# Second norm of a tile issued whole, with the operands of the tile ahead of it in mid-slot; last norms spread to the end

## The chip, the cores and the metric

The kernel runs on one core of one Trainium2 chip. The metric is the device time of one execution in microseconds. Five engines work in parallel, each in the order of its own instruction stream: TensorE (PE, with its weight loads shown apart as PEld), VectorE (DVE), ScalarE (ACT), GpSimd (POOL) and SyncE (SP), which issues the transfers here.

## The reference

One decoder layer for a prompt of 2048 rows and a sample group of 8 × 4 = 32 rows, which share the weights. The model width is 1024 (`D`). After the attention heads and the spatial-gating units, which this change does not touch, come

```
x = x + concat(att, u * gate) @ w_out                  # output projection, residual
h = rmsnorm(x, norm2_g)
x = x + (silu(h @ w_gate) * (h @ w_up)) @ w_down       # SwiGLU, width 2816
y = rmsnorm(x, final_g)
rmsnorm(x, g) = x * rsqrt(mean(x * x) + eps) * g
```

All of it is in fp32; the kernel returns `y` and the key, value and gating caches.

## The kernel before, in words

The 2048 rows are 16 row tiles of 128 rows (`P`), the sample group is one tile of 32. They go through the output projection, the second norm and the SwiGLU in three blocks: 6 tiles, 6 tiles, and 4 tiles with the sample tile ahead of them. Precise fp32 products are made of three matmuls each, of operands that are split into a high and a low part (`hi`, `lo`): the high part is a copy in the multiplier's format on ACT, the low part a subtraction on DVE or POOL. The products of the SwiGLU and of the last projection go through a seven-product scheme for 2 × 2 blocks, so that their operands are also sums and differences of quarters.

**The second phase.** For each block, `second_phase` (L2167) goes once over the block's tiles in an `order`; one turn is called a slot here. In slot k, PE computes the second half of the output projection of tile `order[k]`: twice 12 matmuls (`out_part`, L1436 to L1438) into one PSUM bank `ps_o`. Around them stands `norm2_slot` (L1545), which is issued at the start of the slot and takes two tiles on by one stage each:

- the tile of one slot ago, `order[k-1]`, has its *norm* done: the bank is added to the residual (`out_end`, L1447, DVE; where the first half of the projection is still in its bank, that is added first), POOL multiplies by the gain (L1473), ACT squares and sums (L1480 or L1483), DVE makes the mean (L1456, L1457), ACT the root (L1458), DVE a Newton step (L146 to L150), and ACT scales the tile in place (L1488);
- the tile of two slots ago, `order[k-2]`, becomes *operands* (`Operands`, L1490): PE transposes its eight 128 × 128 pieces into two PSUM banks `ps_t` (L1500), and ACT and DVE (POOL for one subtraction) make from them the sums and the high and low parts. `first` holds L1514 to L1520, `second` the first split (L139, POOL's L142) and L1525, `third` the second split (L139, DVE's L142), `last` the subtraction L1533, which is the last to read the second bank.

The two are issued in an interleaved order: eviction and gain, transposes and `first`, square, `second`, mean, root and Newton step, `third`, scaling, `last`. `ps_t` takes its banks in turn from a ring of two, so the next tile's transposes need the bank that L1533 reads last.

At each half slot `tick()` runs the jobs that were put there by `later(...)`: the weights of the coming SwiGLU are copied to the high part on ACT (`high`, L1619) and subtracted on POOL (`low_half`, L1623). After the last slot, one more `norm2_slot` and the last tile's operands run within the SwiGLU's first steps.

**The last projection.** `Down` multiplies with `w_down` and makes the final norm. Its `run` goes over steps n; at each, `split` prepares the operands of three steps later (L1883 and L1884 on ACT, L1885 and L1886 on DVE), `mats` issues 12 matmuls, and `queue` holds the norm steps of finished tiles (`late_half`, L1940): square, mean, root, scaling of one half with the gain (DVE), scaling of the other half (ACT), output (SP). For the last four even tiles (`quick`) the six steps stand at n + 1, 2, 2, 3, 3, 4. The last three steps are done by `tail` (L1995), one row tile m after the other (PE order by m); then come the four last odd tiles with their eviction (L1920), square (L1927), mean, root, Newton step, scaling (L2017 on ACT, L2018 on DVE with the gain) and two transfers each, one tile after the other.

Of the kernel before, what the change touches and what calls it, by code (L numbers as in the profile page):

```python
# [10 lines left out]
F32 = mybir.dt.float32  # L11
F32R = mybir.dt.float32r
AF = mybir.ActivationFunctionType
OP = mybir.AluOpType
# [5 lines left out]
P = 128  # L20
T = 2048
NT = T // P
D = 1024
# [11 lines left out]
EPS = 1e-6  # L35
# [31 lines left out]
def hymba_step(ctx: ExitStack, tc: tile.TileContext, A: dict, O: dict):  # L67
# [110 lines left out]
    def zn_tile():  # L178
        return rp.tile([P, 512], F32, name="zn", tag="zn", bufs=3)
# [1264 lines left out]
    def out_end(B, i, half, ps):  # L1444
        hs = slice(half * 512, (half + 1) * 512)
        if B.rows[i] == P:
            dve.tensor_add(B.acc[i][:, hs], B.acc[i][:, hs], ps)  # L1447
# [12 lines left out]
    def rms_c(s1, n):  # L1460
        v, r = s1[:n, 1:2], s1[:n, 2:3]
        newton(r, v)
        return r
# [6 lines left out]
    def norm2_gain(B, i):  # L1470
        n = B.rows[i]
        B.xn[i] = square_tile() if n == P else fa.tile([P, D], F32, name="xns", tag="acc5")
        pool.tensor_mul(B.xn[i][:n], B.acc[i][:n], gain[0][:n])  # L1473
# [12 lines left out]
    def norm2_scale(B, i, r):  # L1486
        n = B.rows[i]
        act.activation(B.xn[i][:n], B.xn[i][:n], AF.Copy, scale=r)  # L1488
# [46 lines left out]
    def place_staged(B):  # L1535

        for z, eng in enumerate((act, dve)):
# [4 lines left out]
            else:  # L1542
                act.activation(dst, src, AF.Copy)

    def norm2_slot(B, k, order):  # L1545

        n = len(order)
        cur = order[k - 1] if 1 <= k <= n else None
        x = None
        if k == n and B.last:  # L1550
            place_staged(B)
        if cur is not None:
            if cur in B.open:
# [272 lines left out]
    class Down:  # L1826
# [95 lines left out]
        def behind(self, k, fn, *args):  # L1922
            self.queue.setdefault(self.n + k, []).append((fn, args))

        def square(self, i, c):
            x = self.acc[i][:, c * 512:(c + 1) * 512]
            act.activation(zn_tile(), x, AF.Square, accum_out=self.sq[i][:, (0, 3)[c == i % 2]:][:, 0:1])  # L1927

        def early_half(self, i):

            self.sq[i] = self.p2.tile([P, 4], F32, name="sq", tag="sq", bufs=8)
            c = i % 2
            x = self.acc[i][:, c * 512:(c + 1) * 512]
            self.behind(1, self.square, i, c)
            self.behind(1, pool.tensor_mul, x, x, gain[1][:, c * 512:(c + 1) * 512])

        def late_half(self, i, quick=False):
            steps = (1, 2, 2, 3, 3, 4) if quick else (1, 2, 3, 4, 5, 6)
            for k, fn in zip(steps, (self.late_square, self.mean, self.root, self.scale, self.scale_rest, self.out)):
                self.behind(k, fn, i)  # L1940

        def late_square(self, i):
            self.square(i, 1 - i % 2)

        def mean(self, i):
            s1 = self.sq[i]
            dve.tensor_scalar(s1[:, 0:1], s1[:, 0:1], s1[:, 3:4], None, op0=OP.add)
            dve.tensor_scalar(s1[:, 1:2], s1[:, 0:1], 1.0 / D, EPS, op0=OP.mult, op1=OP.add)

        def root(self, i):  # L1950
            act.activation(self.sq[i][:, 2:3], self.sq[i][:, 1:2], AF.Sqrt)

        def scale(self, i):
            r = rms_c(self.sq[i], P)
            cs = slice((1 - i % 2) * 512, (2 - i % 2) * 512)
            x = self.acc[i][:, cs]
            dve.scalar_tensor_tensor(x, x, r, gain[1][:, cs], op0=OP.mult, op1=OP.mult)

        def scale_rest(self, i):
            x = self.acc[i][:, i % 2 * 512:(i % 2 + 1) * 512]  # L1960
            act.activation(x, x, AF.Copy, scale=self.sq[i][:, 2:3])

        def out(self, i):
            for c in (i % 2, 1 - i % 2):
# [3 lines left out]
        def run(self):  # L1968
            self.queue = {}
            for n in range(2 * NS - TAIL):  # L1970
                self.n = n
                hv, s, j = self.at(n)
                tick()
                self.sums(n + 3)
                self.split(n + 3)
                self.load(n + 6)
                if s in (0, 2) and j in (5, 8):
                    self.acc_loads(hv, s // 2, j // 8)
                if s > 2 and n % 2 == 0 and n < NS + 5 * NJ:
                    roll(1)  # L1980
                self.mats(n)
                wide = not (hv and s == 6)
                m = j // 2 if wide else j
                if n >= NJ and m < 4 and not (wide and j % 2):
                    phv, ps_, _ = self.at(n - j - 1)
                    self.evict(phv, ps_, m, self.prev)
                    i = phv * 8 + 2 * m
                    if ps_ in (1, 4):
                        self.early_half(i + ps_ // 4)
                    elif ps_ in (5, 6):  # L1990
                        self.late_half(i + ps_ - 5, not wide)
                for fn, args in self.queue.pop(n, ()):
                    fn(*args)  # L1993
                if j == NJ - 1:
                    self.prev = self.banks  # L1995
            self.tail()

        def tail(self):
            n0 = 2 * NS - TAIL
            for _ in range(4):  # L2000
                tick()
            for n in sorted(self.queue):
                for fn, args in self.queue[n]:
                    fn(*args)

            def begin(m):
                i = 8 + 2 * m + 1
                self.mean(i)
                self.root(i)

            def root_end(m):
                return rms_c(self.sq[8 + 2 * m + 1], P)

            def finish(m, r):
                i = 8 + 2 * m + 1
                x = self.acc[i]
                act.activation(x[:, 512:], x[:, 512:], AF.Copy, scale=r)  # L2017
                dve.scalar_tensor_tensor(x[:, 0:512], x[:, 0:512], r, gain[1][:, 0:512], op0=OP.mult, op1=OP.mult)  # L2018
                self.out(i)
# [12 lines left out]
            begin(3)  # L2032
            finish(3, root_end(3))

    def second_part(B, h):

# [36 lines left out]
    gain = []  # L2073
# [21 lines left out]
    def open_end(B, i):  # L2095
        out_end(B, i, 0, B.open.pop(i))
# [379 lines left out]
```

## Time and profile before

| | |
|---|---|
| runs, median of 3 | 2480.85 us (2478.23 to 2482.76) |
| profiled execution | 2477.78 us, its span 2476.0 us |
| mean granted clock of PE | 0.993 of full speed |
| busy share of the span | PE 97%, PEld 86%, DVE 68%, ACT 49%, POOL 49% |
| the places of the change | second phases: 943.9 to 984.5 us, 1372.8 to 1401.6 and 1782.5 to 1803.8 (block 0, 1, 2); the end: 2447 to 2476 us |

A line of the timeline gives start and duration in us, engine, line of the kernel, operation, output<-inputs, form and count; in brackets stands the idle time just before, with the engine, tile and line that ended it. A matmul of 128 × 512 shows 0.39 us, since matmuls overlap; their starts are some 0.23 us apart. The trace is of one execution, so sums are made against its own time.

### The profile page before, as it was taken

The numbers are of one execution on the slowest core, as the hardware profiler recorded it, in microseconds if no ns is written. First come the engines' busy times: TensorE is split into PE (matmuls) and PEld (weight loads), VectorE is DVE, ScalarE is ACT, GpSimd is POOL, SyncE is SP. The second block draws the span as 40 slices with busy tenths as digits, with TensorE's granted clock in tenths as the row PEclk, the third lists the DMA queues.
The fourth block names the chain that finished last, engine by engine and source line by source line (L and its number), as shares of the span: only waits on it lengthen the run. The fifth ranks groups of instructions, "written<-read, shape, count | busy, mean of one in ns | idle before, by whom it ended". The sixth has DMA issues, their size and how long they took to land. (4 is left out here: it accounts for less than half of the span.)

```text
span 2476.0 us, 39227 instructions
## 1 busy us (share of the span) xinstructions
PE 2394.6 (97%) x13358; PEld 2123.2 (86%) x13358; DVE 1694.0 (68%) x3093; ACT 1223.0 (49%) x2421; POOL 1209.2 (49%) x921
## 2 busy tenths in 40 slices
PE   8999999999989889999999999999999999999997
PEld 7787787778888777999998899999799998888886
DVE  4369786446878777655665687776567666877886
ACT  6424344546877666433333533334455554445544
POOL 1145653224575756666664576667468872100100
PEclk9999999999999999999999999999999999999999
DMA  8873854788788765566669166766747676766842
GB/s 265 250 209 114 285 146 144 238 278 266 231 281 260 226 179 179 178 212 212 207 204 312 46 238 246 258 233 220 264 145 235 220 229 250 267 197 234 297 135 88
DMA packets 316949, 537.17 MB, mean 217 GB/s; under 512 B 28609, under 2 KB 151906, under 8 KB 310862
## 3 DMA queue, kind: packets, MB, share of 16 engines
q1 hardware_dynamic: 311788, 526.16, 64.8%
q10 hardware_dynamic: 4962, 8.51, 1.2%
q8 instruction: 106, 1.74, 0.3%
q14 instruction: 93, 0.76, 0.1%
HBM read 418.41 MB, written 186.28 MB: 244 GB/s over the span
## 5 line engine op out<-in xcount | busy, mean ns | idle before, releaser
L1686 PE MATMUL ps_m<-xh,op 128*128 128x384 f32 (+5 forms) x1932 | 612.2, 317 | 0.3 <-DVE raw L1723 0.2
L1687 PE MATMUL ps_m<-xl,op 128*128 128x384 f32 (+5 forms) x1932 | 611.9, 317 | 0.0
L1688 PE MATMUL ps_m<-xh,op 128*128 128x384 f32 (+5 forms) x1932 | 611.3, 316 | 0.0
L1623 POOL TENSOR_TENSOR op<-fr,op 128x512 fp32r<-128x512 f32 x286 | 403.2, 1426 | 90.0 <-ACT op L1619 67.3
L1686 PEld LDWEIGHTS ps_m<-xh,op 128*128 128x128 f32 x1932 | 363.9, 188 | 1.6 <-DVE raw L1723 0.6
L1687 PEld LDWEIGHTS ps_m<-xl,op 128*128 128x128 f32 x1932 | 363.8, 188 | 0.6
L1688 PEld LDWEIGHTS ps_m<-xh,op 128*128 128x128 f32 x1932 | 364.2, 189 | 0.0
L1623 POOL TENSOR_TENSOR op<-pair,op 128x512 fp32r<-128x512 f32 x126 | 169.0, 1342 | 157.3 <-DVE hr L1748 85.0
L335 PE MATMUL ps_s<-wh,xh 128*128 128x512 f32 x480 | 196.2, 409 | 6.2 <-ACT xh L139 6.2
L1619 ACT ACTIVATE op<-fr 128x512 fp32r<-128x512 f32 x330 | 196.5, 621 | 9.7 <-DMA fr<-ab_d 5.8
L336 PE MATMUL ps_s<-wl,xh 128*128 128x512 f32 x480 | 190.1, 396 | 0.0
L337 PE MATMUL ps_s<-wh,xl 128*128 128x512 f32 x480 | 189.8, 395 | 0.0
L1737 ACT ACTIVATE ps_t<-zn 128x384 f32<-128x384 f32 (+2 forms) x132 | 60.0, 454 | 249.7 <-DVE zn L1716 204.9
L1883 ACT ACTIVATE op<-fr 128x512 fp32r<-128x512 f32 x140 | 88.7, 634 | 181.7 <-issue 88.0
L1993 POOL TENSOR_TENSOR ac<-ac,final_g 128x512 f32<-128x512 f32 x12 | 19.5, 1622 | 319.6 <-ACT zn L1927 252.7
L1885 DVE TENSOR_TENSOR op<-fr,op 128x512 fp32r<-128x512 f32 x140 | 102.2, 730 | 75.3 <-ACT op L1883 75.2
L1619 ACT ACTIVATE op<-pair 128x512 fp32r<-128x512 f32 x126 | 79.0, 627 | 110.2 <-DVE pair L1609 110.2
L335 PEld LDWEIGHTS ps_s<-wh,xh 128*128 128x128 f32 x480 | 91.9, 191 | 34.6 <-issue 7.3
L337 PEld LDWEIGHTS ps_s<-wh,xl 128*128 128x128 f32 x480 | 91.7, 191 | 20.5 <-DVE xl L142 0.2
L1900 PE MATMUL ps_m<-op 128*128 128x512 f32 x280 | 108.9, 389 | 0.0
L1901 PE MATMUL ps_m<-op 128*128 128x512 f32 x280 | 108.9, 389 | 0.0
L1902 PE MATMUL ps_m<-op 128*128 128x512 f32 x280 | 108.9, 389 | 0.0
(553 smaller groups left out, 5965.0 us busy)
## 6 DMA issues: line engine op xcount, KB each, us to landing
fr<-in_w_gate_dram SPq DMA_DIRECT2D x132, 256.0 KB
out_ks_dram<-in_cache_k_dram SPq DMA_DIRECT2D x56, 512.0 KB
out_vs_dram<-in_cache_v_dram SPq DMA_DIRECT2D x56, 512.0 KB
fr<-in_w_up_dram SPq DMA_DIRECT2D x110, 256.0 KB
fr<-ab_d SPq DMA_DIRECT2D x88, 256.0 KB
a<-h_d SPq DMA_DIRECT2D x80, 256.0 KB
fr<-t_d SPq DMA_DIRECT2D x80, 256.0 KB
raw<-in_w_in_dram SPq DMA_DIRECT2D x72, 256.0 KB
```

The costliest lines, as they stand in the source:

```text
L335: pe.matmul(o[j], xh[:, k, :], wh, start=(k == 0), stop=False)
L336: pe.matmul(o[j], xh[:, k, :], wl, start=False, stop=False)
L337: pe.matmul(o[j], xl[:, k, :], wh, start=False, stop=(k == KD - 1))
L1619: act.activation(ops[f, j][0], ab[f][j], AF.Copy)
L1623: (eng or pool).tensor_sub(lo_, ab[f][j], hi.bitcast(F32))
L1686: pe.matmul(out, wh[:, ks], xh[:, :, k], start=(k == 0), stop=False)
L1687: pe.matmul(out, wh[:, ks], xl[:, :, k], start=False, stop=False)
L1688: pe.matmul(out, wl[:, ks], xh[:, :, k], start=False, stop=(k == 3))
L1885: dve.tensor_sub(wl, w, wh.bitcast(F32))
L1900: pe.matmul(banks[m], hh[:, ts], wh, start=first, stop=False, skip_group_check=more)
L1901: pe.matmul(banks[m], hh[:, ts], wl, start=False, stop=False, skip_group_check=more)
L1902: pe.matmul(banks[m], hl[:, ts], wh, start=False, stop=j == NJ - 1, skip_group_check=more)
```

## The change

1. `second_phase`: in all slots but the last, the interleaved `norm2_slot` is replaced. At the start of slot k, `norm2_sum` issues the whole norm of `order[k-1]`; between the two halves of 12 matmuls `norm2_operands` issues the transposes and the whole operands of `order[k-2]`. The last slot and the call after it keep `norm2_slot`.
2. `Down.late_half`: without `quick`, every tile has one step per n, at n + 1 to n + 6.
3. `tail`: the four last odd tiles are taken in pairs. Their sums lie beside each other in one tile `[P, 4, 2]`, and mean, root and Newton step are done on 128 × 2 elements (`roots(0)`, `roots(2)`). POOL multiplies the low columns by the gain after the square, DVE then scales them alone; most outputs move behind the last matmuls.

```diff
+    def norm2_sum(B, cur):
+        if cur in B.open:
+            open_end(B, cur)
+        out_end(B, cur, 1, B.half1.pop(cur))
+        norm2_gain(B, cur)
+        s1, more = norm2_square(B, cur, None)
+        rms_b(s1, B.rows[cur], more)
+        norm2_scale(B, cur, rms_c(s1, B.rows[cur]))
+
+    def norm2_operands(B, i):
+        x = Operands(B, i)
+        x.first()
+        x.second()
+        x.third()
+        x.last()
...
         def early_half(self, i):
 
-            self.sq[i] = self.p2.tile([P, 4], F32, name="sq", tag="sq", bufs=8)
+            if i < 8 or i % 2 == 0:
+                self.sums_tile(i)
+            elif i % 4 == 1:
+                self.sums_tile(i, i + 2)
...
-        def late_half(self, i, quick=False):
-            steps = (1, 2, 2, 3, 3, 4) if quick else (1, 2, 3, 4, 5, 6)
-            for k, fn in zip(steps, (self.late_square, self.mean, self.root, self.scale, self.scale_rest, self.out)):
-                self.behind(k, fn, i)
+        def late_half(self, i):
+            for k, fn in enumerate((self.late_square, self.mean, self.root, self.scale, self.scale_rest, self.out)):
+                self.behind(k + 1, fn, i)
...
-            r = {}
             for m in range(4):
                 for n in range(n0, 2 * NS):
                     self.mats(n, (m,))
-                if m:
-                    begin(m - 1)
-                    r[m - 1] = root_end(m - 1)
-                self.evict(1, 6, m, self.Y)
-                self.late_square(8 + 2 * m + 1)
-                if m:
-                    finish(m - 1, r[m - 1])
-            begin(3)
-            finish(3, root_end(3))
+                sum_up(m)
+                if m == 1:
+                    roots(0)
+                    self.scale_rest(tile_of(0))
+                elif m == 3:
+                    self.scale_rest(tile_of(1))
+                    for y in range(2):
+                        scale_low(y)
+                        self.out(tile_of(y))
+                    roots(2)
+            scale_low(2)
+            self.scale_rest(tile_of(2))
+            self.out(tile_of(2))
+            scale_low(3)
+            x = self.acc[tile_of(3)][:, 512:]
+            dve.tensor_scalar(x, x, self.col(tile_of(3), 2), None, op0=OP.mult)
+            self.out(tile_of(3))
...
     def second_phase(B, order, after=None):
 
         for k, i in enumerate(order):
-            norm2_slot(B, k, order)
+            apart = k < len(order) - 1
+            if not apart:
+                norm2_slot(B, k, order)
+            elif k:
+                norm2_sum(B, order[k - 1])
             B.half1[i] = ps = ps_o()
             for c in range(2):
                 tick()
+                if c and apart and k > 1:
+                    norm2_operands(B, order[k - 2])
                 if c and k > 2 and i in B.open:
                     first_end(B, i)
                 out_part(B, i, 1, range(c * 4, c * 4 + 4), ps, c == 0, c == 1)
```

The new functions in `tail` are these (`newton` is the Newton step, L146 to L155):

```diff
+            def sum_up(m):
+                self.evict(1, 6, m, self.Y)
+                self.late_square(tile_of(m))
+                x = low_columns(m)
+                pool.tensor_mul(x, x, gain[1][:, 0:512])
+
+            def roots(m):
+                t_ = self.sq[tile_of(m)][0]
+                dve.tensor_add(t_[:, 0], t_[:, 0], t_[:, 3])
+                dve.tensor_scalar(t_[:, 1], t_[:, 0], 1.0 / D, EPS, op0=OP.mult, op1=OP.add)
+                act.activation(t_[:, 2], t_[:, 1], AF.Sqrt)
+                newton(t_[:, 2], t_[:, 1])
```

The order of ACT's instructions in block 0, from slot 2 on, before (`acc_9962` is the second tile, whose norm this is; `ps_t_10274` and `ps_t_10279` hold the first tile's transposes; `s` are the sums):

```order
L1619 ACTIVATE op<-raw 128x512
L1514 ACTIVATE zn<-ps_t_10274 128x256
L1515 ACTIVATE xh_9950<-ps_t_10274 128x256
L1480 ACTIVATE xh_9950,s_10108<-acc_9962 128x512
L139 ACTIVATE xh_9950<-zn 128x512
L1525 ACTIVATE xh_9950<-ps_t_10279 128x512
L1458 ACTIVATE s_10108<-s_10108 128x1
L139 ACTIVATE xh_9950<-zn 128x512
L1488 ACTIVATE pair<-pair,s_10108 128x1024
L1619 ACTIVATE op<-fr 128x512 x2
```

And ACT in the changed kernel, at the same place (the first tile's transposes are now in `ps_t_10303` and `ps_t_10308`; the copies are now L1635):

```order
L1635 ACTIVATE op<-raw 128x512
L1480 ACTIVATE xh_9950,s_10108<-acc_9962 128x512
L1458 ACTIVATE s_10108<-s_10108 128x1
L1488 ACTIVATE pair<-pair,s_10108 128x1024
L1635 ACTIVATE op<-fr 128x512 x2
L1514 ACTIVATE zn<-ps_t_10303 128x256
L1515 ACTIVATE xh_9950<-ps_t_10303 128x256
L139 ACTIVATE xh_9950<-zn 128x512
L1525 ACTIVATE xh_9950<-ps_t_10308 128x512
L139 ACTIVATE xh_9950<-zn 128x512
L1483 ACTIVATE xh_9950,s_10348<-acc_10267 128x1024
```

The norm's three instructions (L1480, L1458, L1488) stood between those of the operands; now they stand together ahead of the operands, with the weight copies between the two, and the next norm (L1483, third tile) begins behind the operands' last. DVE's rows move alike: eviction, mean and Newton step of a tile come together, ahead of L1516 to L1533.

At the end of the program, DVE's last evictions (L1920 before, L1936 now) and what stands between them, before:

```order
L1920 TENSOR_TENSOR acc_18494<-acc_18494,ps_o_24394 128x512
L2018 SCALAR_TENSOR_TENSOR ac<-ac,sq,final_g 128x512
L1947 TENSOR_SCALAR sq<-sq 128x1
L1948 TENSOR_SCALAR sq<-sq 128x1
L146 RECIPROCAL sq<-sq 128x1
L148 TENSOR_SCALAR sq<-sq 128x1
L149 TENSOR_SCALAR sq<-sq 128x1
L150 TENSOR_SCALAR sq<-sq 128x1
L1920 TENSOR_TENSOR acc_18570<-acc_18570,ps_o_24395 128x512
```

And now:

```order
L1936 TENSOR_TENSOR acc_18494<-acc_18494,ps_o_24394 128x512
L1936 TENSOR_TENSOR acc_18570<-acc_18570,ps_o_24395 128x512
L2052 TENSOR_SCALAR ac<-ac,sq 128x512 x2
L2045 TENSOR_TENSOR sq<-sq 128x2
L2046 TENSOR_SCALAR sq<-sq 128x2
L146 RECIPROCAL sq<-sq 128x2
```

The last two evictions (tiles `acc_18494`, `acc_18570`) follow each other; the small operations of their norms come once, on two columns, behind the scaling of the two tiles before.

More of the change, by code (lines that the diff above doesn't have):

```diff
@@ L1923, in behind, with col, sums_tile @@
             self.queue.setdefault(self.n + k, []).append((fn, args))
+        def col(self, i, k):
+            t_, y = self.sq[i]
+            return t_[:, k, y:y + 1]
+        def sums_tile(self, *tiles):
+            t_ = self.p2.tile([P, 4, 2], F32, name="sq", tag="sq", bufs=8)
+            for y, i in enumerate(tiles):
+                self.sq[i] = t_, y
         def square(self, i, c):
             x = self.acc[i][:, c * 512:(c + 1) * 512]
-            act.activation(zn_tile(), x, AF.Square, accum_out=self.sq[i][:, (0, 3)[c == i % 2]:][:, 0:1])
+            act.activation(zn_tile(), x, AF.Square, accum_out=self.col(i, (0, 3)[c == i % 2]))
         def early_half(self, i):
-            self.sq[i] = self.p2.tile([P, 4], F32, name="sq", tag="sq", bufs=8)
+            if i < 8 or i % 2 == 0:
+                self.sums_tile(i)
+            elif i % 4 == 1:
+                self.sums_tile(i, i + 2)
             c = i % 2
@@ L1945, in mean @@
         def mean(self, i):
-            s1 = self.sq[i]
-            dve.tensor_scalar(s1[:, 0:1], s1[:, 0:1], s1[:, 3:4], None, op0=OP.add)
-            dve.tensor_scalar(s1[:, 1:2], s1[:, 0:1], 1.0 / D, EPS, op0=OP.mult, op1=OP.add)
+            dve.tensor_scalar(self.col(i, 0), self.col(i, 0), self.col(i, 3), None, op0=OP.add)
+            dve.tensor_scalar(self.col(i, 1), self.col(i, 0), 1.0 / D, EPS, op0=OP.mult, op1=OP.add)
         def root(self, i):
-            act.activation(self.sq[i][:, 2:3], self.sq[i][:, 1:2], AF.Sqrt)
+            act.activation(self.col(i, 2), self.col(i, 1), AF.Sqrt)
         def scale(self, i):
-            r = rms_c(self.sq[i], P)
+            newton(self.col(i, 2), self.col(i, 1))
             cs = slice((1 - i % 2) * 512, (2 - i % 2) * 512)
             x = self.acc[i][:, cs]
-            dve.scalar_tensor_tensor(x, x, r, gain[1][:, cs], op0=OP.mult, op1=OP.mult)
+            dve.scalar_tensor_tensor(x, x, self.col(i, 2), gain[1][:, cs], op0=OP.mult, op1=OP.mult)
         def scale_rest(self, i):
             x = self.acc[i][:, i % 2 * 512:(i % 2 + 1) * 512]
-            act.activation(x, x, AF.Copy, scale=self.sq[i][:, 2:3])
+            act.activation(x, x, AF.Copy, scale=self.col(i, 2))
         def out(self, i):
@@ L1990, in run @@
                     elif ps_ in (5, 6):
-                        self.late_half(i + ps_ - 5, not wide)
+                        self.late_half(i + ps_ - 5)
                 for fn, args in self.queue.pop(n, ()):
@@ L2004, in tail, with low_columns, scale_low @@
                     fn(*args)
[L2006 to L2019, printed above, removed]
-            r = {}
+            tile_of = lambda m: 8 + 2 * m + 1
+            def low_columns(m):
+                return self.acc[tile_of(m)][:, 0:512]
+            def sum_up(m):
[9 more added lines that the diff above has]
+                newton(t_[:, 2], t_[:, 1])
+            def scale_low(m):
+                x = low_columns(m)
+                dve.tensor_scalar(x, x, self.col(tile_of(m), 2), None, op0=OP.mult)
             for m in range(4):
```

## The prediction

> **What bounds the kernel now.** I read the page's first part, then TensorE's waits, then the timeline of the places that the change touches.
>
> ```profile
> span 2476.0 us, 39227 instructions
> ...
> PE 2394.6 (97%) x13358; PEld 2123.2 (86%) x13358; DVE 1694.0 (68%) x3093; ACT 1223.0 (49%) x2421; POOL 1209.2 (49%) x921
> ...
> PE ps_t L1500 <- ACT pair L1488: 3.6, 4, 1.5
> PE ps_t L1900 <- ACT op L1884: 3.2, 2, 2.7
> ...
> PE ps_t L1500 <- ACT xns L1488: 1.4, 1, 1.4
> ...
> PE ps_t L1500 <- DVE xl L1533: 0.3, 1, 0.3
> ```
>
> TensorE (PE) sets the time: it is busy for 97% of the span. A wait row reads: who waits <- for whom: total us, times, longest. PE's waits at the transposes (L1500) are 3.6 + 1.4 + 0.3 = 5.3 us over three blocks, and in the tail (L1900) 3.2 us. That is all that the change can take away directly. Whatever PE newly waits for is added to the end one for one. So the question is how long a round of ScalarE (ACT) and VectorE (DVE) lasts against a slot of PE.
>
> ```profile
> 955.02 1.03 PE L1500 MATMUL ps_t<-ident,pair 128*128 128x128 f32 x8
> 961.48 1.36 PE L1500 MATMUL ps_t<-ident,pair 128*128 128x128 f32 x8
> ...
> 976.15 1.38 PE L1500 MATMUL ps_t<-ident,pair 128*128 128x128 f32 x8 [1.29 <-ACT pair L1488]
> 983.64 1.09 PE L1500 MATMUL ps_t<-ident,pair 128*128 128x128 f32 x8 [0.54 <-ACT pair L1488]
> ```
>
> The timeline of block 0 (start, duration, engine, line): from one tile's transposes to the next, 961.48 − 955.02 = 6.46 us, are a slot: 1.03 of transposes and 24 matmuls, so (6.46 − 1.03)/24 = 0.226 each. PE needs no more, yet waits 1.29 once. Why:
>
> ```profile
> 976.08 0.68 DVE L1533 TENSOR_TENSOR xl<-ps_t,xh 128x512 fp32r<-128x512 f32 x1
> 976.68 0.67 DVE L1447 TENSOR_TENSOR acc<-acc,ps_m 128x512 f32<-128x512 f32 x1
> ...
> 982.43 1.15 ACT L1488 ACTIVATE pair<-pair,s 128x1024 f32<-128x1024 f32 x1 [0.52 <-DVE s L150]
> 982.86 0.68 DVE L1533 TENSOR_TENSOR xl<-ps_t,xh 128x512 fp32r<-128x512 f32 x1
> ```
>
> From one L1533, the last operation of a tile's operands, to the next one 982.86 − 976.08 = 6.78 us pass: that is today's round on ACT and DVE, in which the norm of one tile and the operands of the tile ahead of it fill each other's gaps. It is 0.3 longer than a slot.
>
> **The change part by part.** First, both chains alone. The first norm of the block has no operands beside it, and the last operands have no norm:
>
> ```profile
> 949.65 0.69 DVE L1447 TENSOR_TENSOR acc<-acc,ps_o 128x512 f32<-128x512 f32 x1 [1.55 <-PE ps_o L1438]
> ...
> 952.86 1.16 ACT L1488 ACTIVATE pair<-pair,s 128x1024 f32<-128x1024 f32 x1 [1.04 <-POOL pair L1473]
> 953.92 0.62 ACT L1619 ACTIVATE op<-fr 128x512 fp32r<-128x512 f32 x1
> ...
> 955.22 0.69 DVE L1447 TENSOR_TENSOR acc<-acc,ps_o 128x512 f32<-128x512 f32 x1 [0.40 <-PE ps_o L1438]
> ```
> ```profile
> 991.17 0.39 ACT L1514 ACTIVATE zn<-ps_t 128x256 f32<-128x256 f32 x1 [0.54 <-PE ps_t L1500]
> ...
> 993.89 0.60 ACT L1525 ACTIVATE xh<-ps_t 128x512 fp32r<-128x512 f32 x1 [0.22 <-DVE zn L1520]
> ...
> 996.43 0.61 ACT L139 ACTIVATE xh<-zn 128x512 fp32r<-128x512 f32 x1
> 997.08 0.69 DVE L142 TENSOR_TENSOR xl<-zn,xh 128x512 fp32r<-128x512 f32 x1 [2.17 <-ACT xh L139]
> 997.69 0.68 DVE L1533 TENSOR_TENSOR xl<-ps_t,xh 128x512 fp32r<-128x512 f32 x1
> ```
>
> Norm: 953.92 − 949.65 = 4.27 us, to where ACT is free. Operands: 993.89 − 991.17 = 2.72 to L1525; L1525 itself 0.60; the second L139 to the subtraction L142, 0.65; L142 to L1533, 0.61; L1533, 0.68: together 5.26.
>
> Now the order. In the new slot, ACT has the norm's square, root and scaling, then the weight copies (L1619, now L1635), and only then L1514; DVE has the whole norm ahead of the operands. Both engines run their rows in this order, so L1514 waits behind L1488, and the next norm's eviction (L1447) waits behind L1533. The chains that overlapped stand in series: 4.27 + copies + 5.26, and 0.60 (976.08 to 976.68) for the eviction of the next tile's first half where that is due. That is 10 to 11 us against 6.46. PE feels it at the transposes: the two PSUM banks of the ring are free only when L1533 has read the second. Copies:
>
> ```profile
> 961.11 1.13 ACT L1619 ACTIVATE op<-fr 128x512 fp32r<-128x512 f32 x2
> ...
> 1372.77 1.04 PE L1500 MATMUL ps_t<-ident,pair 128*128 128x128 f32 x8
> ...
> 1401.55 1.03 PE L1500 MATMUL ps_t<-ident,pair 128*128 128x128 f32 x8
> ...
> 1782.54 0.67 DVE L1447 TENSOR_TENSOR acc<-acc,ps_o 128x512 f32<-128x512 f32 x1
> 1803.78 1.03 PE L1500 MATMUL ps_t<-ident,pair 128*128 128x128 f32 x8
> ```
>
> Two take 1.13. The count of copies in each round is that of the order of ACT's rows. *Block 0* (six tiles, from the second norm's eviction at 955.22): first round 4.27 + 1.13 + 5.26 = 10.66, to 965.88; second 0.60 + 10.66, to 977.14; third, one copy, 0.60 + 4.27 + 0.57 + 5.26 = 10.70, to 987.84. The last slot has the old form and needs the old interval from the end of L1533 (976.08 + 0.68 = 976.76) to the transposes it leads to (983.64): 6.88. So those start at 994.72: **+11.1**. PE's own path, from the freed bank over half the transposes (0.52) and 24 matmuls (5.43), gives 993.79, 0.93 less.
>
> *Block 1*: the eviction stands 0.20 behind the transposes of 1372.77, as in block 0: 1372.97. First halves were evicted earlier, so no 0.60; two, one and no copies: 10.66 + 10.10 + 9.53, to 1403.26. The last interval without 0.60 is 6.28: 1409.54 against 1401.55, **+8.0** (PE's own path 0.33 less).
>
> *Block 2* (sample tile first, five units, hence two rounds): 1782.54 + 4.27 + four copies 2.26 + 2.63 (the sample's operands go by half the columns; half of 5.26, an estimate) = 1791.70; + 10.10 = 1801.80; + 6.28 = 1808.08 against 1803.78: **+4.3** (0.33 less).
>
> **The clock.** After an idle time PE runs slower for a while:
>
> ```profile
> 1782.70 0.68 PE L1500 MATMUL ps_t<-ident,xns 32*128 32x32 f32 x8 [1.41 <-ACT xns L1488]
> ...
> 1784.15 0.63 PE L1436 MATMUL ps_o<-woh,xh 128*128 128x512 f32 x1
> ...
> 1787.53 0.40 PE L1438 MATMUL ps_o<-wol,xl 128*128 128x512 f32 x1
> ```
>
> Eight matmuls (1784.15 to 1787.53) take 3.38 instead of 8 × 0.226 = 1.81: 1.5 to 1.6 lost. By the sums above PE would reach the last slot's transposes of block 0 at 977.14 + 0.52 + 12 × 0.226 = 980.4, and the second bank is free at 987.84: over 7 us of idle time, and by the same working 6.3 in block 1 and 6.9 in block 2. (The idle times ahead of these fall into waits anyway.) 3 × 1.5 = 4.5, of which 0.93 + 0.33 + 0.33 = 1.6 is hidden beside ACT's longer path: **+2.9**.
>
> The Trainium skill ("TensorE: Matmul & The Clock Gate", Part 1, on the clock gate) puts the drop to half rate after an idle window of about 3.4 us. The trace differs: 1.41 us of idle already led to spacings of 0.42 us. By the page three stalls would cost 3 × 1.7 (3.4 us at half rate) less the hidden 1.6, 3.5 instead of 2.9.
>
> **The tail.**
>
> ```profile
> 2452.16 0.39 PE L1902 MATMUL ps_t<-op 128*128 128x512 f32 x1
> 2453.02 0.51 PE L1900 MATMUL ps_t<-op 128*128 128x512 f32 x1 [0.47 <-ACT op L1884]
> ...
> 2457.03 0.79 PE L1900 MATMUL ps_t<-op 128*128 128x512 f32 x1 [2.70 <-ACT op L1884]
> ...
> 2465.08 0.39 PE L1902 MATMUL ps_o<-op 128*128 128x512 f32 x1
> ...
> 2468.47 0.68 DVE L1920 TENSOR_TENSOR acc<-acc,ps_o 128x512 f32<-128x512 f32 x1
> ...
> 2471.70 0.72 ACT L2017 ACTIVATE acc<-acc,sq 128x512 f32<-128x512 f32 x1 [1.04 <-DVE sq L150]
> ```
>
> PE waits for the last splits because ACT and DVE carry two rounds of the `quick` norms ahead of them. With one step per round that goes: 33 matmuls after 2452.16 at 0.227 end their starts at 2459.65 instead of 2465.08, **−5.4** (the slow spacing after 2457.03 included). If ACT stays late, 0 of it comes. Behind the last matmul (2465.08 + 0.39 = 2465.47 to 2476.0, 10.5 us) the last eviction waited for other tiles' norms until 2468.47. Now it follows at once: 0.1, then 3.23 from eviction to scaling as in the old chain (2468.47 to 2471.70), 0.2 for GpSimd's product, three DVE scalings of the two last tiles (not in the trace; between half and the whole of the 0.68 of L1920, I take 0.63: 1.9), and the last output, 2476.0 − 2472.42 = 3.6. That is about 9.0: **−1.5**. The outputs now come close together, eight for the four odd tiles:
>
> ```profile
> out_yp_dram<-ac SPq DMA_DIRECT2D x8, 256.0 KB
> ```
>
> Bunched, they can give these 1.5 back.
>
> **Sum.** 11.1 + 8.0 + 4.3 + 2.9 − 6.9 = +19.4. On the profiled time, 2477.78 + 19.4 = 2497.2. The median of the three runs, 2480.85, is 3.1 above the profiled one; so 2500.3, and I say 2500. *Bounds:* if the copies (2.83 + 1.70 + 2.83 = 7.4) hide in the chains' own gaps and the clock costs nothing, +9.1: 2490; with the tail's gain larger by 3, 2487. Upwards:
>
> ```profile
> 959.87 1.59 DVE L142 TENSOR_TENSOR xl<-zn,xh 128x512 fp32r<-128x512 f32 x1
> ```
>
> Beside a GpSimd subtraction L142 took 1.59 instead of 0.61 to its successor; in all eight rounds that is +7.8. With no gain behind the last matmul, 2500.3 + 7.8 + 1.5 = 2510.
>
> **The rivals.**
> *Faster (0.08).* The transposes in mid-slot find finished operands, and no round exceeds 6.46 us: PE's 5.3 us of waits and one slow spell (1.5) go, and the tail's 6.9: 2480.85 − 13.7 = 2467. For it: in block 0's stretch DVE and ACT have room:
>
> ```profile
> 943.89:984.49 40.60, 38.54 (x186) 30.90 (x184) 29.47 (x73) 27.91 (x57) 29.55 (x18) 1.00 0.54 176
> ```
>
> (us, then busy time of PE, PEld, DVE, ACT, POOL): 29.5 and 27.9 of 40.6. Against it: the room is inside the chains, and a serial order cannot use it. It decides at a round of 6.46.
>
> *About the same (0.07).* Half of the overlap survives, for example because GpSimd and DVE finish early; a round of about 8.0: block 0 loses 3 × (8.0 − 6.46) = 4.6, less the 2.8 that its four slots lost already (983.64 − 955.02 = 28.62, against 4 × 6.46): +1.8. Three such blocks are +5.4 at most, a slow spell 1.5, the tail −6.9: 2480.85, no change. Against it: 4.27 + 5.26 has no part that can run under the other.
>
> *Slower still (0.20).* DVE's L142 meets GpSimd in every round and stalls grow as in the upper bound: 2510.
>
> *The tail does not gain (0.10).* PE still waits there, since the even tiles' last steps are only moved behind other splits: 2500 + 6.9 = 2507.
>
> **How the numbers follow.** My forecast gets 0.55; the two slower rivals 0.30. About 0.2%, 5 us, is what a measurement can tell from no change. Faster 0.08, same 0.07, slower 0.85. The range 2487 to 2512 holds the forecast with its bounds and both slower rivals; left out are the two on the other side.
>
> **What would show it.** In the changed trace: L1500 waits for L1533 with a total of 20 us or more in place of 0.3; the distance from one L1533 to the next of 10 to 11 us in the early slots; spacings of 0.42 after the idle times; no wait at the tail's matmuls (L1916 in the new numbering, L1900 before); the last eviction within 0.5 us of the last matmul. Wrong would be a distance of 6.5 to 8 between the L1533, or PE waiting for something other than the ring's banks.

## The result and the profile after

The changed kernel takes 2503.69 us (median of 4 runs, 2500.9 to 2507.94), the kernel before 2481.81 us (2478.23 to 2483.71): a ratio of 1.0091, 95% interval 1.007 to 1.0113, or 17 to 28 us slower. The profiled execution has a span of 2499.1 us against 2476.0, with PE's mean granted clock at 0.989 instead of 0.993. The forecast was 2500, range 2487 to 2512, chance of slower 0.85.

PE's waits at the transposes, in the view of waits of the changed kernel (who waits <- for whom: total us, times, longest):

```profile
PE ps_t L1500 <- DVE xl L1533: 17.1, 7, 3.0
...
PE ps_t L1500 <- DVE xl L1517: 5.7, 4, 2.7
...
PE ps_t L1500 <- DVE xst L1533: 0.7, 1, 0.7
```

Together 23.5 us, where it was 5.3. The releaser changed too: before, PE waited for the scaled tile (L1488), now it waits for a bank that the operands still read. The timeline of block 0 shows one round of the changed kernel, from the last operation of one tile's operands (L1533) to that of the next:

```profile
965.96 0.68 DVE L1533 TENSOR_TENSOR xl<-ps_t,xh 128x512 fp32r<-128x512 f32 x1
966.56 0.68 DVE L1447 TENSOR_TENSOR acc<-acc,ps_m 128x512 f32<-128x512 f32 x1
967.15 0.68 DVE L1447 TENSOR_TENSOR acc<-acc,ps_o 128x512 f32<-128x512 f32 x1
967.87 1.06 ACT L1483 ACTIVATE xh<-acc 128x1024 fp32r<-128x1024 f32 x1 [2.55 <-DVE acc L1447]
...
970.50 1.15 ACT L1488 ACTIVATE pair<-pair,s 128x1024 f32<-128x1024 f32 x1 [1.06 <-DVE s L150]
971.56 1.24 ACT L1635 ACTIVATE op<-raw 128x512 fp32r<-128x512 f32 x2
972.70 0.36 ACT L1514 ACTIVATE zn<-ps_t 128x256 f32<-128x256 f32 x1
974.54 0.63 ACT L139 ACTIVATE xh<-zn 128x512 fp32r<-128x512 f32 x1 [1.21 <-DVE zn L1518]
975.39 0.60 ACT L1525 ACTIVATE xh<-ps_t 128x512 fp32r<-128x512 f32 x1 [0.22 <-DVE zn L1520]
975.89 0.62 ACT L139 ACTIVATE xh<-zn 128x512 fp32r<-128x512 f32 x1
976.54 0.69 DVE L142 TENSOR_TENSOR xl<-zn,xh 128x512 fp32r<-128x512 f32 x1 [1.24 <-ACT xh L139]
977.15 0.68 DVE L1533 TENSOR_TENSOR xl<-ps_t,xh 128x512 fp32r<-128x512 f32 x1
...
977.98 1.09 PE L1500 MATMUL ps_t<-ident,pair 128*128 128x128 f32 x4 [3.03 <-DVE xl L1533]
```

977.15 − 965.96 = 11.19 us, against a slot of 6.46. Read it from top to bottom: with the small operations left out, each row starts about where the row above it lets it, now on DVE, now on ACT, and the brackets show how long the row's own engine had stood idle (2.55, 1.06, 1.21, 1.24). In the kernel before, those gaps held the other tile's work. GpSimd has a part in the chain too. In this round its gain product (L1473, 967.91 to 970.32) ended 0.06 us ahead of the Newton step. In the other seven rounds the scaling (L1488) waited for that product, 1.04 to 1.34 us. The stages, in the view of windows (start and end, length, then busy time of PE, PEld, DVE, ACT, POOL, and PE's clock), before:

```profile
955.22:983.64 28.42, 26.36 (x129) 20.89 (x127) 23.47 (x60) 21.56 (x46) 23.99 (x15) 1.00 0.43 140
1372.97:1401.55 28.58, 26.41 (x128) 20.91 (x127) 22.66 (x57) 19.72 (x43) 20.96 (x13) 1.00 0.21 65
1782.54:1803.78 21.24, 20.95 (x96) 16.91 (x97) 14.44 (x44) 14.89 (x35) 15.19 (x10) 0.92 0.45 149
```

and after, between the same instructions:

```profile
956.25:996.80 40.55, 31.41 (x129) 24.74 (x127) 23.41 (x60) 22.72 (x48) 23.05 (x15) 0.83 0.28 98
1385.88:1423.76 37.88, 29.51 (x128) 23.21 (x127) 20.47 (x57) 20.05 (x43) 21.43 (x13) 0.91 0.15 49
1804.73:1830.96 26.23, 20.25 (x92) 15.80 (x91) 13.54 (x44) 15.07 (x35) 15.13 (x10) 0.87 0.37 121
```

The blocks grew by 12.1, 9.3 and 5.0 us, with no more work on DVE and at most 1.2 us more on ACT in them, and PE's clock fell from 1.00 (0.92) to 0.83, 0.91 and 0.87.

At the end PE has no wait any more. From the last block's last transposes (1810.01 before, 1837.19 after) to the start of the last matmul (2465.08 and 2486.84) it takes 649.65 instead of 655.07 us, −5.4; from there to the end of the span 12.26 instead of 10.92 us, +1.3. Four rows around that last stretch of the changed kernel:

```profile
2483.94 2.55 POOL L2041 TENSOR_TENSOR ac<-ac,final_g 128x512 f32<-128x512 f32 x2 [28.84 <-ACT zn L1952]
...
2485.30 1.22 DVE L2046 TENSOR_SCALAR sq<-sq 128x2 f32<-128x2 f32 x1
...
2489.25 2.67 POOL L2041 TENSOR_TENSOR acc<-acc,final_g 128x512 f32<-128x512 f32 x2 [2.76 <-ACT zn L1952]
...
2490.72 1.21 DVE L2045 TENSOR_TENSOR sq<-sq 128x2 f32<-128x2 f32 x1
```

An addition of two elements per row takes 1.21 us on DVE. It ends at 2491.93, and GpSimd's two products end at 2489.25 + 2.67 = 2491.92. The scalar operation at 2485.30 ends at 2486.52, and the two products before it at 2486.49.

The rest of the 23.1 us is +1.0 ahead of the first block, where nothing is changed. That part scatters: the second norm's eviction of block 0 stood between 948.6 and 967.9 us in the profiles of these studies whose second phase is that of the kernel before. So stretches of traces are compared below between fixed instructions: the tail from the last block's last transposes to the end of the span (before 665.99, after 661.91).

### The profile page after: what moved, and what is told of

The parts are those of the page before. It is cut to its first block, busy times and chain, and to the rows that moved or that the text cites. A ratio compares the mean times of both kernels' runs of the same rounds, so it can differ in the third digit from the quotient of the medians.

```text
span 2499.1 us, 39234 instructions
## 1 busy us (share of the span) xinstructions
PE 2401.3 (96%) x13358; PEld 2128.0 (85%) x13358; DVE 1690.3 (68%) x3084; ACT 1223.5 (49%) x2418; POOL 1212.4 (49%) x925
## 5 line engine op out<-in xcount | busy, mean ns | idle before, releaser
L1635 ACT ACTIVATE op<-fr 128x512 fp32r<-128x512 f32 x330 | 196.6, 621 | 11.6 <-DMA fr<-ab_d 7.0
L1635 ACT ACTIVATE op<-pair 128x512 fp32r<-128x512 f32 x126 | 79.0, 627 | 111.2 <-DVE pair L1625 111.2
```

The costliest lines, as they stand in the source:

```text
L1635: act.activation(ops[f, j][0], ab[f][j], AF.Copy)
```

## The experiments

**Each part alone.** The first kernel has the new `second_phase` and the old end, the second the new end and the old `second_phase`.

```diff
-            norm2_slot(B, k, order)
+            apart = k < len(order) - 1
+            if not apart:
+                norm2_slot(B, k, order)
+            elif k:
+                norm2_sum(B, order[k - 1])
...
+                if c and apart and k > 1:
+                    norm2_operands(B, order[k - 2])
```
```diff
-        def late_half(self, i, quick=False):
-            steps = (1, 2, 2, 3, 3, 4) if quick else (1, 2, 3, 4, 5, 6)
+        def late_half(self, i):
...
+                sum_up(m)
+                if m == 1:
+                    roots(0)
+                    self.scale_rest(tile_of(0))
...
```

> Only part 1 of the change (second phase); the end of the program is that of the kernel before. Theory A (in the second phase the two chains stand in series on ACT and DVE, a round of 10 to 11 us against a slot of 6.46) puts the whole loss here and a small gain at the end: the changed kernel is 23 us longer in its profiled span, of which about 26 belong to the three blocks and -4 to the tail, so this kernel should be +25 to +28 over the kernel before, with waits of L1500 for L1533 and L1517 of about 23 us. Rival: the loss comes in part from the end of the program (the last matmul to the end grew from 10.5 to 11.9 us); then this kernel is less than +20.

> Only parts 2 and 3 of the change (last norms spread, tail in pairs with g on GpSimd); the second phase is that of the kernel before. By the traces: no wait of PE in the tail (-5.4), but 11.9 instead of 10.5 us behind the last matmul (+1.4): -4.0 in all. The forecast on record had -6.9 for it. Rival (the tail does not gain): within 1 us of the kernel before.

Measured against the kernel before of the same chip: e1 2510.28 us, ratio 1.0116 (1.0098 to 1.0134), +29 us; e2 2474.24 us, 0.9974 (0.9963 to 0.9985), −6.5 us. In the traces, e1's stretch from block 0's second eviction (959.17) to the last transposes (1839.76) is 25.8 us longer than before (955.22 to 1810.01) and its tail 666.24 us; e2's tail is 661.89, −4.1. The two effects have opposite signs, and each is alone about what it is in the whole change (26 us longer and 4.1 shorter there, between the same instructions): the new end is a gain that the second phase hides.

**Wholeness or place?** The change does two things to the second phase: it makes both chains whole, and it moves the operands to mid-slot. Two kernels with the old end separate them: e3 issues whole norm and then whole operands at the start of the slot (the edit is against e1), e4 the old interleaved form in mid-slot (against the kernel before).

```diff
                 norm2_sum(B, order[k - 1])
+                if k > 1:
+                    norm2_operands(B, order[k - 2])
...
-                if c and apart and k > 1:
-                    norm2_operands(B, order[k - 2])
```
```diff
-            norm2_slot(B, k, order)
+            apart = k < len(order) - 1
+            if not apart:
+                norm2_slot(B, k, order)
...
                 tick()
+                if c and apart:
+                    norm2_slot(B, k, order)
```

> The second phase with whole norm and, behind it, whole operands, both issued at the start of the slot as the old interleaved form was; nothing in mid-slot; the old end. Theory A (series): the round is the same, norm + copies + operands, so +20 to +28 as with the transposes in mid-slot; the distance of one L1533 to the next 10 to 11 us. Rival B (the place in mid-slot is what costs, because the bank is given back half a slot later than the next transposes ask for it): within 5 us of the kernel before.

> The old interleaved form, issued in mid-slot between the two groups of 12 matmuls in all slots but the last; the old end. Theory A (series): the round stays at 6.8 us, and only the step from mid-slot to the start of the last slot can cost up to 2 us in each block: 0 to +6. Rival B (place in mid-slot): +20 or more.

e3: 2509.54 us, ratio 1.0122 (1.0103 to 1.0141), +30 us, slightly above what was expected. e4: 2488.69 us, 1.0029 (1.0017 to 1.0042), +7 us. The timeline of DVE in block 0 of e3, and of e4:

```profile
966.43 0.68 DVE L1533 TENSOR_TENSOR xl<-ps_t,xh 128x512 fp32r<-128x512 f32 x1
977.55 0.68 DVE L1533 TENSOR_TENSOR xl<-ps_t,xh 128x512 fp32r<-128x512 f32 x1
989.54 0.68 DVE L1533 TENSOR_TENSOR xl<-ps_t,xh 128x512 fp32r<-128x512 f32 x1
```
```profile
964.85 0.68 DVE L1533 TENSOR_TENSOR xl<-ps_t,xh 128x512 fp32r<-128x512 f32 x1
972.05 0.68 DVE L1533 TENSOR_TENSOR xl<-ps_t,xh 128x512 fp32r<-128x512 f32 x1
980.04 0.68 DVE L1533 TENSOR_TENSOR xl<-ps_t,xh 128x512 fp32r<-128x512 f32 x1
986.82 0.68 DVE L1533 TENSOR_TENSOR xl<-ps_t,xh 128x512 fp32r<-128x512 f32 x1
```

Whole chains have rounds of 11.1 and 12.0 us here, issued at the start of the slot, as against 11.2 and 10.4 in mid-slot in the changed kernel; interleaved ones in mid-slot stay at 6.8 to 8.0. The loss comes from the series, not from the place. Mid-slot costs some 7 us of its own, slightly above what was expected: in each block PE waits once for L1488 where the last slot takes its place at the start again (2.5 to 3.4 us).

**A smaller dose (e9).** One step of the old form is moved: the scaling ahead of the second split.

```diff
+        if cur is not None:
+            norm2_scale(B, cur, r)
         if x:
             x.third()
-        if cur is not None:
-            norm2_scale(B, cur, r)
```

> The kernel before with one step of the interleaved form moved: the norm's scaling (L1488) ahead of the operands' second split (L139, L142) instead of behind it; nothing else. Theory A (a round lasts as long as the waits of one chain are not filled by the other): ACT now waits for the Newton step with nothing to do, the second L139 comes behind the 1.15 us of the scaling, L1533 about 1.2 us later; rounds of about 8.0 instead of 6.8 us, over 4 + 4 + 3 rounds, with slow spells of PE: +9 to +17. Rival (only whole sequences in series hurt; there is room of a quarter on both engines, so one step moved costs nothing): within 3 us of the kernel before.

2496.27 us, ratio 1.0065 (1.0042 to 1.0087), +16 us, over half of the 29 us that the new second phase costs alone, from the place of one instruction. The timeline:

```profile
963.21 0.16 DVE L146 RECIPROCAL s<-s 128x1 f32<-128x1 f32 x1 [0.51 <-ACT s L1458]
...
964.21 1.15 ACT L1488 ACTIVATE pair<-pair,s 128x1024 f32<-128x1024 f32 x1 [1.04 <-DVE s L150]
965.27 0.61 ACT L139 ACTIVATE xh<-zn 128x512 fp32r<-128x512 f32 x1
...
965.92 0.69 DVE L142 TENSOR_TENSOR xl<-zn,xh 128x512 fp32r<-128x512 f32 x1 [1.80 <-ACT xh L139]
966.53 0.68 DVE L1533 TENSOR_TENSOR xl<-ps_t,xh 128x512 fp32r<-128x512 f32 x1
...
974.32 0.68 DVE L1533 TENSOR_TENSOR xl<-ps_t,xh 128x512 fp32r<-128x512 f32 x1
```

ACT waits 1.04 us for the Newton step with its next work (L139) ready behind L1488, then DVE waits 1.80 us for that L139. The next rounds are 7.79 us (966.53 to 974.32), and up to 9.8 later. PE's waits at L1500 are 13.4 us for L1533 and 5.3 for L1488. The more a chain stands alone, the longer the round in block 0: 6.1 to 8.6 us before, 7.8 to 9.8 here, 10.4 to 11.2 in the changed kernel.

**The weight copies.** They were a term of 7.4 us in the sum. e5 is e1 with a slot's first set of jobs ahead of the norm:

```diff
         for k, i in enumerate(order):
+            tick()
...
             for c in range(2):
-                tick()
+                if c:
+                    tick()
```

> The second phase of the changed kernel with the first of a slot's two sets of weight jobs issued ahead of the norm instead of behind it; old end. About one ACT copy in each round moves from the place between norm and operands to the place ahead of the norm's square, where ACT has 2.5 us of idle time. Theory A with the copies as a term of the series: some 0.57 less in each of 7 rounds, 3 to 4 us less than part 1 alone over the three blocks. If the copies are no term (or what moves with them holds up DVE and GpSimd ahead of the norm): no change.

A miss: 2507.18 us in its single run, a span of 2505.4 (e1: 2506.0) with block 0 beginning some 7 us earlier than in e1. From the first transposes (954.94) to the last (1839.17) it takes 884.2 us, in e1 (961.76 to 1839.76) 878.0: 6 us more, not 3 to 4 less. The jobs bring a GpSimd subtraction along, which now runs ahead of the gain product, and the scaling waits for that product:

```profile
953.23 1.29 POOL L1639 TENSOR_TENSOR op<-raw,op 128x512 fp32r<-128x512 f32 x1
...
954.47 2.39 POOL L1473 TENSOR_TENSOR pair<-acc,norm_g 128x1024 f32<-128x1024 f32 x1
...
956.90 1.15 ACT L1488 ACTIVATE pair<-pair,s 128x1024 f32<-128x1024 f32 x1 [1.95 <-POOL pair L1473]
```

The experiment moved more than the copies, so the size of their term is not settled by it. The trace of the changed kernel shows it: in the round above L1635 fills 971.56 to 972.70 between L1488 and L1514, with no gap on either side, and block 1 has a round with one copy and one with none:

```profile
1400.03 1.15 ACT L1488 ACTIVATE pair<-pair,s 128x1024 f32<-128x1024 f32 x1 [1.09 <-POOL pair L1473]
1401.09 0.62 ACT L1635 ACTIVATE op<-fr 128x512 fp32r<-128x512 f32 x1
1401.61 0.36 ACT L1514 ACTIVATE zn<-ps_t 128x256 f32<-128x256 f32 x1
...
1409.83 1.15 ACT L1488 ACTIVATE pair<-pair,s 128x1024 f32<-128x1024 f32 x1 [1.06 <-POOL pair L1473]
1410.88 0.36 ACT L1514 ACTIVATE zn<-ps_t 128x256 f32<-128x256 f32 x1
```

L1514 starts 1.58 and 1.05 us after L1488 does, so a copy delays it by some 0.5 us. Eleven copies stand there in the eight rounds, and together they fill 5.9 us.

**The end.** Four tails, all on the old second phase: the changed one (e2), spreading alone (e6), the changed one with the gain back on DVE (e7), and a rewritten one (e8). The edits in this order, e7's against e2, e8's the loop of its tail, in which `mean` adds up a pair's sums and takes the root, `step` is the Newton step and `scale_low` that of e7:

```diff
-            steps = (1, 2, 2, 3, 3, 4) if quick else (1, 2, 3, 4, 5, 6)
+            steps = (1, 2, 3, 4, 5, 6)
```
```diff
-                x = low_columns(m)
-                pool.tensor_mul(x, x, gain[1][:, 0:512])
...
-                dve.tensor_scalar(x, x, self.col(tile_of(m), 2), None, op0=OP.mult)
+                dve.scalar_tensor_tensor(x, x, self.col(tile_of(m), 2), gain[1][:, 0:512], op0=OP.mult, op1=OP.mult)
```
```diff
+                self.evict(1, 6, m, self.Y)
+                if m == 3:
+                    scale_low(1)
+                self.late_square(tile_of(m))
+                if m == 1:
+                    mean(0)
+                elif m == 2:
+                    step(0)
+                    self.scale_rest(tile_of(0))
+                    self.scale_rest(tile_of(1))
+                    scale_low(0)
+                    self.out(tile_of(0))
+                elif m == 3:
+                    self.out(tile_of(1))
+                    mean(2)
+                    step(2)
+            for m in (3, 2):
+                scale_low(m)
+                self.scale_rest(tile_of(m))
+                self.out(tile_of(m))
```

> Only part 2 of the change: the last even tiles' norm steps at n + 1 to n + 6; second phase and tail are those of the kernel before. Theory (PE waits in the tail because the quick norm steps stand ahead of the last splits on ACT and DVE): no wait of PE there, the stretch from the last block's transposes to the last matmul's start shrinks by 5.4 us as in the changed kernel, and from there to the end it stays at 10.9 us: -5.4 us. Rival (the steps come due later and now delay the odd tiles): the end stretch grows by 1 to 3 us and eats part of it.

> Parts 2 and 3 of the change, but the multiplication by the gain in the tail is back on DVE, in one operation with the scaling; nothing on GpSimd there. In the changed kernel the stretch from the last matmul's start to the end is 12.26 us, and DVE operations of two elements took 0.54, 1.22 and 1.21 us while GpSimd multiplied. Theory P (GpSimd holds DVE up): those take 0.2 us, the stretch shrinks to 10 to 11 us. Rival Q (the pairs themselves cost it, because the first tile of a pair waits for the second): the operations of two elements are short, but the stretch stays at 11.8 us or more.

> A rewritten tail on the second phase of the kernel before: norm steps spread as in part 2, sums in pairs, gain on DVE, each eviction ahead of the small operations of the pair before it, the first pair's scaling done before and beside the last tile's square. From the rows of the trace (eviction 0.68, square 0.82, mean, root and Newton step about 2.0, two scalings 1.5, last output 3.6): about 9.3 us from the last matmul's start to the end instead of 10.9, and -5.4 for PE's wait: -7 us against the kernel before. If the outputs, now close together, hold each other up, the stretch is 10.5 or more and the gain -5 to -6.

| tail | last transposes to last matmul's start, us | from there to the end, us | sum, us | ratio to before (95% interval) |
|---|---|---|---|---|
| before | 655.07 | 10.92 | 665.99 | 1 |
| e6, spread alone | 649.63 | 12.16 | 661.79 | 0.9991 (0.9981 to 1.0002) |
| e2, as in the change | 649.63 | 12.26 | 661.89 | 0.9974 (0.9963 to 0.9985) |
| e7, no GpSimd | 649.66 | 9.71 | 659.37 | 0.9979 (0.9970 to 0.9988) |
| e8, rewritten | 649.66 | 9.51 | 659.17 | 0.9971 (0.9960 to 0.9983) |

Spreading the steps takes PE's waits away, and by the traces all of the gain of the change's end is there: e2's tail is no shorter than e6's. The runs do not show it as clearly: e6's ratio is not told from 1, and it lies 0.0017 above that of e2, which ran on another chip. In e6 the rival held: the old chain, once the matmuls finish earlier, is itself the bound. DVE's evictions in the tail of e6 (the timeline):

```profile
2461.59 0.68 DVE L1920 TENSOR_TENSOR ac<-ac,ps_t 128x512 f32<-128x512 f32 x1
...
2464.66 0.68 DVE L1920 TENSOR_TENSOR acc<-acc,ps_o 128x512 f32<-128x512 f32 x1
...
2467.71 0.68 DVE L1920 TENSOR_TENSOR acc<-acc,ps_o 128x512 f32<-128x512 f32 x1
```

One tile in 3.06 us, while PE makes one in 9 × 0.227 = 2.04. The pairs are to shorten that chain, and in e7 they do, by 2.5 us; GpSimd takes it back in the changed kernel. In e7's timeline the same sums of two elements are short:

```profile
2473.44 0.15 DVE L2027 TENSOR_TENSOR sq<-sq 128x2 f32<-128x2 f32 x1
2473.63 0.17 DVE L2028 TENSOR_SCALAR sq<-sq 128x2 f32<-128x2 f32 x1
```

The intervals of e2, e7 and e8 overlap; their order is shown by the traces alone. e8 gained 6.8 us of the forecast 7 in the trace, 0.9971 in the runs. It is faster than both kernels of this study.

**Contention in the old rounds.** In the kernel before, DVE's L142 took up to 1.59 us beside GpSimd. e10 is e8 with the first low part on DVE too.

```diff
-            split_sb(hi[:, 3:5], lo_[:, 3:5], self.sums[0])
+            split_sb(hi[:, 3:5], lo_[:, 3:5], self.sums[0], eng_lo=dve)
```

> The rewritten tail of the earlier run, and in the operands the first low part (L142) on DVE instead of GpSimd. DVE gets 0.68 us more in each round; GpSimd loses 1.3, so that DVE's second L142 should not meet it any more (1.39 to 1.59 us where it did, 0.69 where it did not). If contention sets the old round: -1 to -4 us against the run with the rewritten tail alone (-7 against the kernel before), by the waits of L1500 for L1488 (3.6 us) and the slow spells behind them. If the order of DVE's work sets it: +2 to +8.

2478.57 us, ratio 0.9988 (0.9978 to 0.9999): some 4 us slower than e8 relative to the kernel before. The stretch from block 0's second eviction to the last transposes is 859.55 us against 854.77 in e8, and PE waits in e10

```profile
PE ps_t L1500 <- ACT pair L1488: 9.7, 11, 2.1
```

instead of 3.6 us. The second L142 no longer met GpSimd (0.68 to 0.70 us), but the one that was moved did: it took 1.08 to 1.75 us in seven tiles, beside a weight subtraction or the gain product. It stands ahead of the mean and the Newton step, which L1488 waits for. So the edit moved the contention to an earlier place as well as adding work, and the run does not tell which of the two, contention or the order of DVE's work, sets the old round.

## Why the prediction was right

| term | forecast, us | trace, us |
|---|---|---|
| block 0, with its share of the clock | 11.1 + 0.6 | 12.1 |
| block 1 | 8.0 + 1.2 | 9.3 |
| block 2 | 4.3 + 1.2 | 5.0 |
| PE's waits in the tail | −5.4 | −5.4 |
| behind the last matmul | −1.5 | +1.3 |
| ahead of block 0 | 0 | +1.0 |
| sum | +19.4 | +23.1 (the rows leave −0.2 elsewhere) |

That the sum comes so near is in part luck. The rounds of block 0 were 0.7 us shorter together than forecast and its last interval, with its share of the clock, 1.1 us longer, and the miss behind the last matmul, 2.8 us, would have been most of the 3.7 us difference alone.

**The serial round was right**, and e3, e4 and e9 show that it is the cause. The rounds forecast for block 0 were 10.66, 11.26 and 10.70 us; from 956.25 they measured 10.39, 11.19 and 10.38 (L1533 ends at 966.64, 977.83 and 988.21). In block 1: 10.66, 10.10, 9.53 against 11.03, 9.83, 9.28. The copies, reckoned at 7.4 us, were 5.9: each took 0.5 us of the path instead of 0.57, and in block 2's first round two of the four ran ahead of the scaling (1804.75 and 1805.89).

**The last interval of a block was mis-sized, with the right total.** The forecast took ACT's old interval, 6.88 us, from the end of L1533 to the next transposes. PE's own path was longer, as the slow clock made it:

```profile
984.70 0.63 PE L1500 MATMUL ps_t<-ident,pair 128*128 128x128 f32 x4 [0.83 <-DVE xl L1517]
...
988.36 1.09 PE L1500 MATMUL ps_t<-ident,pair 128*128 128x128 f32 x4 [3.02 <-DVE xl L1533]
...
989.10 0.78 PE L1436 MATMUL ps_o<-woh,xh 128*128 128x512 f32 x1
...
993.51 0.44 PE L1437 MATMUL ps_o<-wol,xh 128*128 128x512 f32 x1
...
996.80 1.03 PE L1500 MATMUL ps_t<-ident,pair 128*128 128x128 f32 x8
```

From the freed bank to the next transposes, 8.44 us instead of the 5.95 reckoned for PE at full clock: 2.5 lost in block 0. In block 1 (1416.17 to 1423.76) it was 1.6, in block 2 (1823.58 to 1830.96) 1.4. The forecast had 1.5 for each.

**"PE stands still over 7 us" was wrong.** The first of the two banks comes free at L1517, so four of the eight transposes run early and the idle time falls into pieces, 0.83 and 3.02 us ahead of the last slot of block 0. For the same reason the sign "L1500 waits for L1533 with a total of 20 us or more" was met only together with L1517: 17.8 and 5.7 us. The slow spell came nonetheless. The Trainium skill ("TensorE: Matmul & The Clock Gate", Part 1, on the clock gate) puts the loss of the full clock behind an idle window of about 3.4 us. By these rows, pieces of at most 3.03 us sufficed.

**Behind the last matmul the step that failed is "3.23 from eviction to scaling as in the old chain".** In the changed kernel the last eviction starts 1.0 us behind the last matmul's end, where the forecast had 0.1 and looked for 0.5 at most, since DVE's sums of the first pair were held up by GpSimd. From it to the scaling 5.2 us pass (about 2488.3 to 2493.45), and the last output takes 4.3 instead of 3.6. Without the product (e7) the eviction starts 0.03 us behind and 3.60 us pass to the scaling. The sum had the two engines side by side at no cost, with 0.2 us for GpSimd's product. The Trainium skill states the rule ("SBUF — State Buffer", "Who interferes with whom"): a DVE instruction with two SBUF inputs contends with a GpSimd instruction that reads SBUF, and so does DVE in its two-port modes, while one with a single SBUF input outside these does not. The trace agrees: both short operations end with GpSimd's product, and without it (e7) they take 0.15 and 0.17 us. The addition (L2045) reads two inputs. The other (L2046) reads one, as does the scaling L2052, of which one took 1.55 us beside the product and the rest 0.48; by that rule these ran in a two-port mode, which no row shows.

**The rivals.** The round did not get below 6.46 us, nor to 8.0, so neither the faster nor the equal case came. The slower one (L142 beside GpSimd in every round) had the wrong sign: in the rounds of the changed kernel DVE's L142 meets no GpSimd instruction and takes 0.69 us, where it was up to 1.59. That the tail does not gain is half true: −4.1 us instead of −6.9.

What stays open: where the scatter ahead of block 0 comes from, and whether GpSimd or the order of DVE's work sets the round of the kernel before.

## What to carry to other kernels

On engines that run in order, two chains that each hand over between the same two engines should be issued interleaved: their length in series (here 4.3 + 5.3 us and the copies) is the bound when they are written one after the other, though each engine is busy for only 50 to 60% of the stage. Before moving a block of work, take the length of each chain where it runs alone in the trace, and compare their sum, not the busy time, with the slot of the engine that sets the time. An operation moved to GpSimd does not always run beside DVE for nothing: here two DVE operations of 0.15 and 0.17 us waited for its end. Where such operations stand in a chain that sets the time, price the move by the length of the GpSimd instruction.

## What the runs showed of the hardware

A two-element DVE addition took 1.21 us beside a GpSimd product and 0.15 us without it. In block 0 PE ran some ten matmuls at a spacing of 0.43 us instead of 0.23 after idle pieces of 1.35 and 3.03 us, and again after 0.83 and 3.02 us. Moving one 1.15 us instruction on ACT ahead of one of 0.62 us cost 16 us over the 14 tiles whose norm has another tile's operands beside it, some 1.1 us for each.
